# Second MLP matrices: half of the rows by half of the columns of each quarter as seven block products in place of eight

## The chip, the cores and the metric

The kernel runs on one core of a Trainium2 chip. Its time is the device time of one execution in microseconds (us). The engines are TensorE (PE in the profile, with its weight loads PEld beside it), VectorE (DVE), ScalarE (ACT), GpSimd (POOL) and SyncE (SP), which issues the loads. Each works through its own instructions in a fixed order, and waits on the others by semaphores.

## The reference

The reference is a two-layer decoder trunk over 256 tokens of width 2048, in float32: layer 0 has recurrent mixers, layer 1 dilated attention, and each layer ends with an MLP of inner width 8192. The change is in the two MLPs:

```
def squared_relu_mlp(h, w1, w2):
    return jnp.square(jax.nn.relu(h @ w1)) @ w2
...
        h = h + squared_relu_mlp(rms_norm(h, norm_mlp[layer]), mlp_w1[layer], mlp_w2[layer])
```

Here `w1` is 2048 x 8192 and `w2` 8192 x 2048.

## The kernel before

**Precision.** Every large product is made of three passes. A float32 operand is split into `hi`, its rounding to the matmul's type fp32r, and `lo`, the rest, also fp32r; the product is hi x hi + hi x lo + lo x hi. Activations are split by `split_to` (lines 198 to 205), weights by the class `Weights` (85 to 102): ACT casts a half of 1024 columns (line 97) and DVE subtracts it from the raw half (line 98).

**Weight stream.** Weights come in units of 128 x 2048 float32 (1 MB). The list `units` (line 64 on) holds them in the order of use. `unit` (135) hands out the next one and calls `fetch` (104), which issues the load of the unit two further on, on SyncE's queue, and its split. There are three raw tiles (`wraw`, line 46), and five half buffers each for `hi` and `lo` (47, 48). A raw tile is free when its split is done, a half buffer when its last matmul is done.

**The order on the engines.** A scheduler orders every engine's instructions when the program is built: by priority, among those that its own timing says are ready. `stream` moves the loads and splits 150 instructions ahead in priority, `urgent` moves what it encloses 400 ahead (PRIO and URGENT, lines 736 and 737). PE alone keeps the order of the program: `mm` and `turn` (145 to 149) chain every matmul and transpose to the one before.

**The MLP** (`mlp`, line 584) goes by quarters of the inner width, 2048 each. In a quarter, sixteen units of w1 (`project`, 317) give one block of 128 features x 256 tokens each: 16 matmuls of 512 columns and 16 of 256 into one of three PSUM banks "p" (`pmm`, 51). `folded` adds the two halves of the bank, the square of the positive part is taken, and `split_to` writes hi and lo to `bufb[:, m]`. Then come sixteen units of w2, four for each of the four groups n of 512 output columns (`tokens`, 291). There the activations are the stationary operand (128 features x 128 tokens; j is the half of the tokens) and the weights the moving one. A unit has four feature blocks i, two token halves j and three passes: 24 matmuls of 128x512. So a column group takes 96 matmuls into two banks, and a quarter 384. `add_res` (549) then adds each bank, times the token's norm factor, to the residual `xres` on DVE; in the last quarter `Norm.add` takes squares on ACT for the next norm.

**Transposes.** In the last quarter of layer 0, `to_features` (558) appends a job to the list `later`: it transposes the finished 512 columns on PE, four transposes to a bank of the two "pl" banks, which ACT and DVE split with the gain into `bufa`. `flush` (153) runs whatever is in the list, after a unit's matmuls in `tokens` or three quarters through a unit in `project`. With one group finished at a time, eight transposes run at a time.

In layer 1's last quarter the columns are multiplied by the final gain `fing` instead (line 607).

Of the kernel before, what the change touches and what calls it, by code (L numbers as in the profile page):

```python
# [10 lines left out]
F32 = mybir.dt.float32  # L11
F32R = mybir.dt.float32r
# [3 lines left out]
OP = mybir.AluOpType  # L16
# [3 lines left out]
P = 128  # L20
S = 256
D = 2048
KB = D // P
# [17 lines left out]
def trunk_kernel(ctx, tc, x, xtok, cols, tab, masks, pos, fin, w_in, w_gate, w_out, w_qkv, w_o, w1, w2, out):  # L41
    nc = tc.nc
# [33 lines left out]
    for layer in range(2):  # L76
        if layer:
            plan(w_qkv, 48)
            plan(w_o, 16)
        for q in range(4):  # L80
            units.extend((w1, layer * 64 + q * 16 + i) for i in range(16))
            units.extend((w2, layer * 64 + q * 16 + i) for i in range(16))
    at = [0, 0]

    class Weights:
# [18 lines left out]
    def fetch():  # L104
        u = at[0]
        if u >= len(units):
            return
        at[0] += 1
        src, i = units[u]
        with stream():  # L110
            r = wraw.tile([P, 2048], F32, name="raw")
            nc.sync.dma_start(r, src[i])
            made[u] = Weights(r)

    def fetch_first():
        for u in range(4):
# [17 lines left out]

    def unit(src, i):
        u = at[1]
        assert units[u][0] is src and units[u][1] == i, (u, i)
        at[1] += 1
        if u + 2 >= at[0]:
            fetch()  # L140
        return made.pop(u)
# [45 lines left out]

    HA, XA, YA = direct, direct, direct

    def folded(p, name="z", bufs=None):  # L190
        with urgent():
            t = tmp.tile([P, S], F32, name="t1", bufs=2)
            A.copy(t, p[:, S:])  # L193
            z = tmp.tile([P, S], F32, name=name, bufs=bufs)
            V.tensor_tensor(z, p[:, :S], t, OP.add)  # L195
        return z

    def split_to(dst, src, gain=None):
        if gain is None:
            A.copy(dst[:, :S], src)  # L200
            V.tensor_tensor(dst[:, S:], src, dst[:, :S].bitcast(F32), OP.subtract)  # L201
        else:
            A.activation(dst[:, :S], src, AF.Copy, scale=gain)
            V.scalar_tensor_tensor(dst[:, S:], src, gain, dst[:, :S].bitcast(F32),  # L204
                                   op0=OP.mult, op1=OP.subtract)
# [83 lines left out]
            V.scalar_tensor_tensor(r, t, 1.5, r, op0=OP.add, op1=OP.mult)  # L289

    def tokens(src, i0, mov, kgs=(0, 1, 2, 3), by_k=False):
        ps = [pmm.tile([P, 512], F32, name="p") for _ in range(2)]
        for g in kgs:
            w = unit(src, i0 + g)
            order = [(j, i) for i in range(4) for j in range(2)] if by_k else \
                [(j, i) for j in range(2) for i in range(4)]
            for j, i in order:
                k = 4 * g + i
# [239 lines left out]
    for step in ORDER.split():  # L538
# [5 lines left out]
        else:  # L544
            {"x": lru_in, "y": lru_out, "g": lru_gates}[step[0]](i)
    mixers.close()


    def add_res(ps, n, nrm, scale=None):
        at = slice(n * 512, n * 512 + 512)  # L550
        with urgent():
            for j in range(2):
                V.scalar_tensor_tensor(xres[:, j, at], ps[j], 1.0 if scale is None else scale[:, j:j + 1],  # L553
                                       xres[:, j, at], op0=OP.mult, op1=OP.add)
                if nrm:
                    nrm.add(j, n)
# [24 lines left out]
    spot = []  # L581
    spare = cst.tile([P, 1], F32, name="spare")

    def mlp(layer, nrm, nxt, gname):
        r2 = None
        for q in range(4):
            for m in range(16):
                z = folded(project(w1, layer * 64 + q * 16 + m, bufa), "z")
                with urgent():
                    V.scalar_tensor_tensor(z, z, 0.0, z, op0=OP.max, op1=OP.mult)  # L590
                    split_to(bufb[:, m], z)
                if r2 is None:
                    r2 = nrm.inv_mean()
                    if not gname:
                        lut(spare, epsc, AF.Sqrt)
                    spot[:] = [after(V.memset(spare, 0.0), [])]
            for n in range(4):
                ps = tokens(w2, layer * 64 + q * 16 + 4 * n, bufb)
                add_res(ps, n, nxt if q == 3 else None, r2)
                if q == 3:  # L600
                    if gname:
                        to_features(n, gname)
                    else:
                        at = slice(n * 512, n * 512 + 512)
                        with urgent():
                            for j in range(2):
                                V.tensor_tensor(xres[:, j, at], xres[:, j, at], fing[:, at], OP.mult)

    nx1 = Norm()
    mlp(0, nrm, nx1, "nmix1")  # L610


    rot = mixers.enter_context(tc.tile_pool(name="rot", bufs=1))
# [95 lines left out]
    late = ctx.enter_context(tc.tile_pool(name="late", bufs=1))  # L709
    fing = late.tile([P, D], F32, name="fing")  # L710
    nc.sync.dma_start(fing, bass.AP(tensor=fin.tensor, offset=fin.offset, ap=[[0, P], [1, D]]))
    fnorm = Norm()
    mlp(1, nrm, fnorm, None)
    for j in range(2):
# [22 lines left out]
URGENT = 400  # L737
ORDER = "v0 h0 x0 h1 x1 h2 x2 h3 x3 v1 h4 x4 h5 x5 h6 x6 h7 x7 g0 y0 y1 y2 y3 g1 y4 y5 y6 y7"
WARM = 12
NOSYNC = mybir.DependencyInfo(mybir.DependencyClass.NoSync, mybir.DependencyReason.DATA)  # L740


# [23 lines left out]
    return tab, masks  # L766


def _layout(a):
    n = np.asarray  # L770
    blk = lambda w, nb=P: n(w).reshape(w.shape[0] // P, P, w.shape[1] // nb, nb)
# [1 line left out]
    def feat(w):  # L773
        return blk(w).transpose(2, 1, 0, 3).reshape(w.shape[1] // P, P, -1)

    def toks(w):
        b = n(w).reshape(4, 4, P, w.shape[1] // 512, 512)
        return b.transpose(3, 0, 2, 1, 4).reshape(-1, P, 2048)

    colv = lambda v: n(v).reshape(-1, P).T  # L780
# [28 lines left out]
    w2 = np.concatenate([toks(n(w)[q * 2048:q * 2048 + 2048]) for w in a["mlp_w2"] for q in range(4)])  # L809
    tab, masks = _tables()  # L810
    c = np.ascontiguousarray
    return {
# [28 lines left out]
```

## Time and profile before

| what | value |
|---|---|
| median of 3 runs | 2237.01 us (2236.97 to 2237.16) |
| the profiled execution's own time | 2237.57 us |
| its span, first to last instruction | 2235.8 us |
| granted TensorE clock, mean | 0.999 |
| PE busy | 2218.4 us, 99% |
| DVE busy | 1410.6 us, 63% |
| ACT busy | 1074.4 us, 48% |
| loads of raw weights, issue to landing (median) | 4.8 us |
| first MLP, by the windows used below | about 432 to 1142 us |
| second MLP | about 1525 to 2225 us |

A group's row gives the line, the engine, the operation, its output and inputs with shapes, the count, the busy time and the mean length of one, and then the engine's idle time just before such instructions and what ended it. Ends of matmuls are modelled and neighbours overlap, so the distance from one start to the next tells more than the length of one. The chain of waits goes back from the last instruction to what released each step.

### The profile page before, as it was taken

The page shows a single profiled execution, that of the slowest core. Times are in us where ns is not written, and L with a number is a line of the kernel's source. Part 1 is how long each engine was busy: PE and PEld are TensorE (multiplying, and loading weights), DVE is VectorE, ACT ScalarE, POOL GpSimd, SP SyncE. Part 2 cuts the span into 40 slices and gives each one's busy share as a digit, 9 for nine tenths or more (in the row PEclk, how much of TensorE's full clock was granted, in tenths as well). Part 3 has the DMA queues.
Part 4 walks back from the last instruction along what each step waited for, and adds up shares of the span by engine and source line. Part 5 has one row for each costly group of instructions (what it writes and reads, how often), then busy time and mean ns, then how long its engine had stood idle before and what let it go on. Part 6 is the DMA issues. An engine that isn't in the chain of part 4 may idle for free.

```text
span 2235.8 us, 30376 instructions
## 1 busy us (share of the span) xinstructions
PE 2218.4 (99%) x12196; PEld 1935.1 (87%) x12196; DVE 1410.6 (63%) x2220; ACT 1074.4 (48%) x1540; POOL 1.9 (0%) x7
## 2 busy tenths in 40 slices
PE   9999999999999999999999999999999999999998
PEld 8999998888888888888888888888888888888886
DVE  7777886665565565465567878556655645655654
ACT  6444585554444344354554445455434434444543
POOL 0000000000000000000000000000000000000000
PEclk9999999999999999999999999999999999999999
DMA  8444445455555555555554444555555555555553
GB/s 309 151 154 168 152 154 205 172 191 191 200 188 188 190 190 189 199 193 188 188 188 167 172 170 170 191 186 188 189 188 191 191 193 196 189 188 190 190 192 125
DMA packets 58717, 414.51 MB, mean 185 GB/s; under 512 B 6528, under 2 KB 7296, under 8 KB 9168
## 3 DMA queue, kind: packets, MB, share of 16 engines
q1 hardware_dynamic: 58320, 412.20, 51.9%
q8 instruction: 95, 1.56, 0.3%
q0 software_dynamic: 256, 0.38, 0.1%
q14 instruction: 46, 0.38, 0.1%
HBM read 410.70 MB, written 2.10 MB: 185 GB/s over the span
## 4 chain that ended last, share of the span: by engine, by line
PE 98%; ACT 1%; DVE 1%; DMA 0%; issue 0%; SPq 0%; ACTq 0%; DVEq 0%
PE p L146 94%; PE pl L440 1%; PE pl L149 0%; PE pl L665 0%; DMA raw<-in_w_in 0%; PE po L686 0%; PE pd L678 0%; ACT hi L97 0%; DVE bufa L204 0%; ACT L169 0%; DVE lo L98 0%; PE pd L424 0%; PE pl L664 0%; ACT gi L169 0%; PE po L687 0%
## 5 line engine op out<-in xcount | busy, mean ns | idle before, releaser
L98 DVE TENSOR_TENSOR lo<-raw,hi 128x1024 fp32r<-128x1024 f32 (+1 forms) x774 | 932.5, 1220 | 602.7 <-ACT hi L97 435.2
L97 ACT CAST hi<-raw 128x1024 fp32r<-128x1024 f32 (+1 forms) x774 | 811.3, 1049 | 876.7 <-PE p L146 798.7
L146 PE MATMUL p<-bufa,hi 128*128 128x512 f32 (+1 forms) x3840 | 858.2, 357 | 2.4 <-DVE bufa L204 2.4
L146 PE MATMUL p<-hi,bufb 128*128 128x512 f32 x2560 | 792.5, 390 | 0.0
L146 PEld LDWEIGHTS p<-bufa,hi 128*128 128x128 f32 x3840 | 671.9, 189 | 94.8 <-DVE bufa L204 3.5
L146 PEld LDWEIGHTS p<-hi,bufb 128*128 128x128 f32 x2560 | 480.7, 188 | 99.1
L146 PE MATMUL p<-bufa,lo 128*128 128x256 f32 x3200 | 520.0, 284 | 0.0
L146 PE MATMUL p<-lo,bufb 128*128 128x512 f32 x1280 | 498.1, 389 | 0.0
L146 PEld LDWEIGHTS p<-bufa,lo 128*128 128x128 f32 x3200 | 451.9, 191 | 12.3
L146 PEld LDWEIGHTS p<-lo,bufb 128*128 128x128 f32 x1280 | 240.4, 188 | 49.2
L201 DVE TENSOR_TENSOR bufb<-z,bufb 128x256 fp32r<-128x256 f32 x136 | 57.7, 424 | 126.5 <-ACT bufb L200 126.5
L146 PE MATMUL p<-hi,bufa 128*128 128x512 f32 x384 | 122.5, 395 | 0.5 <-ACT hi L97 0.5
L193 ACT COPY t<-p 128x256 f32<-128x256 f32 x128 | 47.6, 372 | 110.0 <-PE p L146 110.0
L146 PEld LDWEIGHTS p<-hi,bufa 128*128 128x128 f32 x384 | 72.2, 188 | 16.1 <-ACT hi L97 1.5
L146 PE MATMUL p<-lo,bufa 128*128 128x512 f32 x192 | 76.4, 398 | 1.6 <-DVE lo L98 1.6
L200 ACT CAST bufb<-z 128x256 fp32r<-128x256 f32 x136 | 54.5, 401 | 17.2 <-DVE z L590 14.4
L553 DVE SCALAR_TENSOR_TENSOR xall<-p,nm,xall 128x512 f32<-128x512 f32 x64 | 47.9, 748 | 19.8 <-PE p L146 19.8
L590 DVE SCALAR_TENSOR_TENSOR z<-z 128x256 f32<-128x256 f32 x128 | 54.5, 426 | 4.4
L195 DVE TENSOR_TENSOR z<-p,t 128x256 f32<-128x256 f32 x128 | 53.5, 418 | 0.0
L258 ACT ACTIVATE z<-xall 128x512 bf16<-128x512 f32 x32 | 20.2, 631 | 53.3 <-DVE xall L553 52.6
L146 PEld LDWEIGHTS p<-lo,bufa 128*128 128x128 f32 x192 | 36.1, 188 | 10.3 <-DVE lo L98 3.6
L440 PE MATMUL pl<-qk 128*128 128x64 f32 x224 | 30.9, 260 | 0.0
(199 smaller groups left out, 730.1 us busy)
## 6 DMA issues: line engine op xcount, KB each, us to landing
raw<-in_w SPq DMA_DIRECT2D x256, 1024.0 KB, 4.8
raw<-in_w_qkv SPq DMA_DIRECT2D x48, 1024.0 KB, 4.8
raw<-in_w_in SPq DMA_DIRECT2D x46, 1024.0 KB, 4.8
raw<-in_w_out SPq DMA_DIRECT2D x16, 1024.0 KB, 4.8
raw<-in_w_o SPq DMA_DIRECT2D x16, 1024.0 KB, 4.8
xall<-in_xtok SPq DMA_DIRECT2D x1, 2048.0 KB, 9.3
raw<-in_w_gate SPq DMA_DIRECT2D x2, 1024.0 KB, 4.8
out<-xall SPq DMA_DIRECT2D x4, 512.0 KB, 3.3
```

Source lines behind the costliest of these rows:

```text
L97: A.copy(h, w)
L98: V.tensor_tensor(l, w, h.bitcast(F32), OP.subtract)
L146: chain[:] = [after(T.matmul(*args, **kw), chain)]
L193: A.copy(t, p[:, S:])
L195: V.tensor_tensor(z, p[:, :S], t, OP.add)
L200: A.copy(dst[:, :S], src)
L201: V.tensor_tensor(dst[:, S:], src, dst[:, :S].bitcast(F32), OP.subtract)
L258: A.activation(q, xres[:, j, n * 512:n * 512 + 512], AF.Square, accum_out=self.ss[:, j, n:n + 1])
L440: T.matmul(pl[:, j], kq[:, js], halves(qp[:, js], c, True), start=True, stop=True)
L553: V.scalar_tensor_tensor(xres[:, j, at], ps[j], 1.0 if scale is None else scale[:, j:j + 1], xres[:, j, at], op0=OP.mult, op1=OP.add)
L590: V.scalar_tensor_tensor(z, z, 0.0, z, op0=OP.max, op1=OP.mult)
```

## The change

In each quarter, the first eight feature blocks (half of the rows of w2) and the first two column groups (half of the columns) are handled together. The activations there are a 2x2 matrix of blocks: two token halves by two sets of four feature blocks, the even ones and the odd ones of the eight (`PAIRED` reorders the rows of w2 accordingly when the inputs are laid out). The weights are a 2x2 matrix as well: two sets of features by two column groups, each block one unit. Their product is made of seven block products of 12 matmuls, by a scheme of Strassen's kind in Winograd's form. The other eight feature blocks of the two groups are multiplied plainly, in four units "n" of 24 matmuls. Groups 2 and 3 stay as they were.

- *Weights.* `plan2` lists eleven operand sets for the pair in the order of `PRODUCTS`; eight load a unit. `combine` makes them. `a` and `t1` are loaded to tiles of their own in the new pool `pair`. DVE then adds in place, in halves of 1024 columns: t1's unit to `a`, then t2's raw unit to `a`, then t2's raw unit to the tile `t1` (t3), then d's raw unit to `a` (t4). Each result is split to hi and lo; `c` is t2's unit split again by itself.
- *Activations.* `sums` makes four sums and differences of each two neighbouring blocks z (DVE, 128x128 each) and splits them into `forms`. The blocks z come from the pool `pair` with three buffers (`zp`).
- *Products.* `products` uses four banks: alpha, delta and gamma of "p", and beta, which is "pd". `after_product` and the ends of the plain units add banks to `xres` by `to_x` on DVE, eight times for the pair where `add_res` made four: beta is added and subtracted in between while its accumulation goes on, and alpha is added to one place after t1 and to another at the end.
- *Transposes.* `to_features` for groups 0 and 1 is called when the pair is complete, so both jobs stand in `later` at the first `flush` of group 2.
- The pool `rot` is opened before the first MLP, since `pair0` comes above it. `T3_DMA` is off.

```diff
@@ the list of units
+    def plan2(i, products):
+        if not products:
+            units.extend((w2, i + u) for u in range(8))
+            return
+        for what, u in PRODUCTS:
+            units.append((w2, None if u is None else i + u, what))
@@ the stream
+    def combine(u, src, i, what):
+        if what in ("a", "t1"):
+            r = held[what] = pair.tile([P, 2048], F32, name=what)
+            nc.sync.dma_start(r, src[i])
+        elif i is not None:
+            r = wraw.tile([P, 2048], F32, name="raw")
+            nc.sync.dma_start(r, src[i])
+            held[what] = r
+        to, add = {"t1": ("a", "t1"), "t2": ("a", "t2"), "t3": ("t1", "t2"), "t4": ("a", "d"),
+                   "a": ("a", None), "c": ("t2", None), "d": ("d", None), "n": ("n", None)}[what]
+        r = held[to]
...
+        for h in range(2):
+            at = slice(h * 1024, h * 1024 + 1024)
+            if add:
+                V.tensor_tensor(r[:, at], r[:, at], held[add][:, at], OP.add)
+            if h == 0:
+                w = made[u] = Weights(r, False)
+            w.split(h * 1024, 1024)
@@ before the MLPs
+    rot = mixers.enter_context(tc.tile_pool(name="rot", bufs=1))
...
+    def sums(k, z1, z2):
+        t = pair.tile([P, 512], F32, name="sums")
+        a11, a21, a12, a22 = z1[:, :P], z1[:, P:], z2[:, :P], z2[:, P:]
+        V.tensor_tensor(t[:, :P], a21, a22, OP.subtract)
+        V.tensor_tensor(t[:, P:2 * P], t[:, :P], a11, OP.subtract)
+        V.tensor_tensor(t[:, 2 * P:3 * P], a11, a21, OP.subtract)
+        V.tensor_tensor(t[:, 3 * P:], a12, t[:, P:2 * P], OP.add)
+        A.copy(forms[:, k, 0], t)
+        V.tensor_tensor(forms[:, k, 1], t, forms[:, k, 0].bitcast(F32), OP.subtract)
+
+    def products(i0, n0, nrm, r2, r2n):
...
+        alpha, delta, gamma = (pmm.tile([P, 512], F32, name="p") for _ in range(3))
+        beta = psc.tile([P, 512], F32, name="po" if n0 else "pd", bufs=1)
...
+        def times(bank, w, get):
+            for i in range(4):
+                h, l = w.part(i * 512, 512)
+                xh, xl = get(i)
+                mm(bank, xh, h, start=not any(b is bank for b in opened), stop=False, skip_group_check=True)
+                opened.append(bank)
+                mm(bank, xh, l, start=False, stop=False, skip_group_check=True)
+                mm(bank, xl, h, start=False, stop=i == 3, skip_group_check=True)
+
+        def to_x(bank, j, n, sign=1, last=False):
+            at = slice(n * 512, n * 512 + 512)
+            with urgent():
+                V.scalar_tensor_tensor(xres[:, j, at], bank, (r2 if sign > 0 else r2n)[:, j:j + 1], xres[:, j, at],
+                                       op0=OP.mult, op1=OP.add)
+                if nrm and last:
+                    nrm.add(j, n)
+
+        after_product = {"a": [(beta, 0, n0, 1)], "t1": [(alpha, 1, n1, 1)], "t2": [(beta, 0, n1, -1)],
+                         "t3": [(beta, 1, n1, -1, True)]}
+        bank = {"a": beta, "t1": alpha, "t2": beta, "c": alpha, "t3": beta, "d": gamma, "t4": beta}
+        for what, u in PRODUCTS:
+            w = unit(w2, None if u is None else i0 + u)
+            if what != "n":
+                times(bank[what], w, side[what])
+                for job in after_product.get(what, ()):
+                    to_x(*job)
+                continue
+            n, g = divmod(u, 4)
+            for j in (1, 0) if n else (0, 1):
+                times({(0, 0): gamma, (0, 1): beta, (1, 0): alpha, (1, 1): delta}[n, j], w,
+                      lambda i, j=j, g=g: plain(j, 4 * g + i))
...
@@ in mlp
-                z = folded(project(w1, layer * 64 + q * 16 + m, bufa), "z")
+                z = folded(project(w1, layer * 64 + q * 16 + m, bufa), "zp", 3, pair)
...
+                if m < 8 and m % 2:
+                    sums(m // 2, zs, z)
+                zs = z
...
             for n in range(4):
-                ps = tokens(w2, layer * 64 + q * 16 + 4 * n, bufb)
-                add_res(ps, n, nxt if q == 3 else None, r2)
+                if n < 2 * PAIRS:
+                    if n % 2 == 0:
+                        products(layer * 64 + q * 16, n, ends, r2, r2n)
+                else:
+                    ps = tokens(w2, layer * 64 + q * 16 + 4 * n, bufb)
+                    add_res(ps, n, ends, r2)
@@ constants
+PAIRS = 1
+T3_DMA = False
+PRODUCTS = (("a", 0), ("t1", 4), ("n", 6), ("t2", 5), ("c", None), ("n", 7), ("t3", None), ("d", 1), ("n", 2),
+            ("t4", None), ("n", 3))
+PAIRED = (0, 2, 4, 6, 1, 3, 5, 7) + tuple(range(8, KB))
```

More of the change, by code (lines that the diff above doesn't have):

```diff
@@ L81, in trunk_kernel @@
             units.extend((w1, layer * 64 + q * 16 + i) for i in range(16))
-            units.extend((w2, layer * 64 + q * 16 + i) for i in range(16))
+            for n in range(0, 4, 2):
+                plan2(layer * 64 + q * 16 + 4 * n, n < 2 * PAIRS)
     at = [0, 0]
@@ L108, in fetch @@
         at[0] += 1
-        src, i = units[u]
+        src, i = units[u][:2]
         with stream():
+            if len(units[u]) > 2:
+                combine(u, src, i, units[u][2])
+                return
             r = wraw.tile([P, 2048], F32, name="raw")
@@ L113, in fetch @@
             made[u] = Weights(r)
+    held = {}
+    def combine(u, src, i, what):
[9 more added lines that the diff above has]
+        r = held[to]
+        if what == "t3" and T3_DMA:
+            nc.gpsimd.dma_start(r, w2[held["c_at"]], accum_op=OP.add)
+            add = None
+        if what == "t2":
+            held["c_at"] = i
+        for h in range(2):
[5 more added lines that the diff above has]
+            w.split(h * 1024, 1024)
     def fetch_first():
@@ L136, in unit @@
         u = at[1]
-        assert units[u][0] is src and units[u][1] == i, (u, i)
+        assert units[u][0] is src and units[u][1] in (None, i), (u, i)
         at[1] += 1
@@ L193, in folded @@
             A.copy(t, p[:, S:])
-            z = tmp.tile([P, S], F32, name=name, bufs=bufs)
+            z = (home or tmp).tile([P, S], F32, name=name, bufs=bufs)
             V.tensor_tensor(z, p[:, :S], t, OP.add)
@@ L291, in tokens @@
     def tokens(src, i0, mov, kgs=(0, 1, 2, 3), by_k=False):
+        ks = PAIRED if src is w2 else range(KB)
         ps = [pmm.tile([P, 512], F32, name="p") for _ in range(2)]
@@ new lines, in products @@
+    def products(i0, n0, nrm, r2, r2n):
+        n1 = n0 + 1
+        i0 += 4 * n0
+        plain = lambda j, k: (bufb[:, k, j * P:j * P + P], bufb[:, k, S + j * P:S + j * P + P])
+        form = lambda f, k: (forms[:, k, 0, f * P:f * P + P], forms[:, k, 1, f * P:f * P + P])
+        side = {"a": lambda i: plain(0, 2 * i), "d": lambda i: plain(0, 2 * i + 1), "t4": lambda i: plain(1, 2 * i + 1),
+                "t1": lambda i: form(0, i), "t2": lambda i: form(1, i), "t3": lambda i: form(2, i),
+                "c": lambda i: form(3, i)}
+        alpha, delta, gamma = (pmm.tile([P, 512], F32, name="p") for _ in range(3))
+        beta = psc.tile([P, 512], F32, name="po" if n0 else "pd", bufs=1)
+        opened = []
+        def times(bank, w, get):
[27 more added lines that the diff above has]
+                      lambda i, j=j, g=g: plain(j, 4 * g + i))
+                if g == 3:
+                    to_x({(0, 0): gamma, (0, 1): beta, (1, 0): alpha, (1, 1): delta}[n, j], j, n + n0, 1, (n, j) != (1, 1))
+            flush()
@@ L591, in mlp @@
                     split_to(bufb[:, m], z)
+                if m < 8 and m % 2:
+                    sums(m // 2, zs, z)
+                zs = z
                 if r2 is None:
                     r2 = nrm.inv_mean()
+                    r2n = tmp.tile([P, 2], F32, name="r2n", bufs=1)
+                    V.tensor_scalar(r2n, r2, -1.0, None, op0=OP.mult)
                     if not gname:
@@ L607, in mlp @@
                                 V.tensor_tensor(xres[:, j, at], xres[:, j, at], fing[:, at], OP.mult)
+    pairs = ExitStack()
+    pair = pairs.enter_context(tc.tile_pool(name="pair0", bufs=1))
+    forms = pair.tile([P, 4, 2, 512], F32R, name="forms")
     nx1 = Norm()
     mlp(0, nrm, nx1, "nmix1")
-    rot = mixers.enter_context(tc.tile_pool(name="rot", bufs=1))
+    pairs.close()
     ppi = rot.tile([32, S], I32, name="ppi")
@@ L711, in trunk_kernel @@
     nc.sync.dma_start(fing, bass.AP(tensor=fin.tensor, offset=fin.offset, ap=[[0, P], [1, D]]))
+    pair = pairs.enter_context(tc.tile_pool(name="pair1", bufs=1))
+    forms = pair.tile([P, 4, 2, 512], F32R, name="forms")
     fnorm = Norm()
     mlp(1, nrm, fnorm, None)
+    pairs.close()
     for j in range(2):
@@ L774, in feat, with toks @@
         return blk(w).transpose(2, 1, 0, 3).reshape(w.shape[1] // P, P, -1)
-    def toks(w):
-        b = n(w).reshape(4, 4, P, w.shape[1] // 512, 512)
+    def toks(w, order=range(KB)):
+        b = n(w).reshape(KB, P, -1)[list(order)].reshape(4, 4, P, w.shape[1] // 512, 512)
         return b.transpose(3, 0, 2, 1, 4).reshape(-1, P, 2048)
@@ L808, in _layout @@
     w1 = np.concatenate([feat(n(w)) for w in a["mlp_w1"]])
-    w2 = np.concatenate([toks(n(w)[q * 2048:q * 2048 + 2048]) for w in a["mlp_w2"] for q in range(4)])
+    w2 = np.concatenate([toks(n(w)[q * 2048:q * 2048 + 2048], PAIRED) for w in a["mlp_w2"] for q in range(4)])
     tab, masks = _tables()
```

5 lines of the change are left out of this document (3 added, 2 removed).

## The prediction

> **What bounds the kernel now.** I read the page's busy times and its chain of waits first, then the busy time by stage in one quarter of the first MLP, then the groups of that stage, then single instructions.
>
> ```profile
> PE 2218.4 (99%) x12196; PEld 1935.1 (87%) x12196; DVE 1410.6 (63%) x2220; ACT 1074.4 (48%) x1540; POOL 1.9 (0%) x7
> PE 98%; ACT 1%; DVE 1%; DMA 0%; issue 0%; SPq 0%; ACTq 0%; DVEq 0%
> ```
>
> TensorE (PE) works nearly all the time and is 98% of the chain that ended last. By stage (window, length, busy PE, PEld, DVE, ACT, POOL, clock, DMA share, GB/s), the first row holds the sixteen units of w1 of a quarter, the second its sixteen units of w2.
>
> ```profile
> 432.00:523.00 91.00, 90.67 (x513) 79.80 (x514) 56.82 (x82) 44.80 (x66) 0.00 (x0) 1.00 0.52 184
> 523.00:610.00 87.00, 87.00 (x393) 72.37 (x392) 44.96 (x41) 34.71 (x34) 0.00 (x0) 1.00 0.54 194
> ```
>
> From the chain in order of time (start, length, what), eight transposes and then 96 matmuls, as many as a column group of w2 has:
>
> ```profile
> 1095.47 0.87 PE pl L149 x8
> 1096.35 21.78 PE p L146 x96
> ```
>
> PE has no idle time in the w2 stage; one matmul of 512 columns takes 21.78 / 96 = 0.2269 us. VectorE (DVE) is busy 45 of 87 us, ScalarE (ACT) 35. What they do there (count, busy us, mean ns, idle before and its releaser):
>
> ```profile
> L98 DVE TENSOR_TENSOR lo<-raw,hi 128x1024 fp32r<-128x1024 f32 x34 | 41.5, 1224 | 42.5 <-ACT hi L97 39.2 <-PE p L146 1.9
> L97 ACT CAST hi<-raw 128x1024 fp32r<-128x1024 f32 x34 | 35.9, 1055 | 53.2 <-PE p L146 51.8 <-DVE z L195 1.5
> L553 DVE SCALAR_TENSOR_TENSOR xall<-p,nm,xall 128x512 f32<-128x512 f32 x8 | 6.0, 748 | 1.6 <-PE p L146 1.6
> ```
>
> ACT waits for PE, and DVE for ACT: the weights are split as far ahead as the five half buffers of each kind allow, two and a half units.
>
> **The matmuls.** The pair of column groups 0 and 1 of a quarter now takes seven products of 12 matmuls and four plain units of 24, 180 in all, where 192 stood. Each of the 12 saved costs 0.2269 us: 2.72 us a quarter, times eight quarters 21.8 us. All of it is on the path, as PE is never idle there. They stay 128x512 on the same kinds of operands, and PE already changes its PSUM bank every 12 matmuls, so I price the rest as before.
>
> [...]
>
> **What VectorE gets in return, in each pair's section.** Two neighbouring operations give the pitch:
>
> ```profile
> 538.82 1.22 DVE L98 TENSOR_TENSOR lo<-raw,hi 128x1024 fp32r<-128x1024 f32 x1 [1.69 <-ACT hi L97]
> 539.96 0.74 DVE L553 SCALAR_TENSOR_TENSOR xall<-p,nm,xall 128x512 f32<-128x512 f32 x1
> 540.62 1.22 DVE L98 TENSOR_TENSOR lo<-raw,hi 128x1024 fp32r<-128x1024 f32 x1
> ```
>
> So 1024 columns occupy DVE 1.14 us and a residual add 0.66. Before, a pair costs 16 splits and 4 residual adds, 20.9 of 43.5 us. After: eleven operand sets, so 22 splits; t1, t2, t3 and t4 each add two halves, 8 adds; eight residual adds for four. No row shows a 128x1024 add with a plain f32 result. At half that width the f32 product with fing (L607) takes 689 ns and the fp32r split (L98) 688, so the type of the result costs nothing; I take 1.14, with the whole duration of 1.22 as the other end. Sum: 30 x 1.14 + 8 x 0.66 = 39.5 us, in a section that PE now crosses in 40.8. This is close (42.0 us at the other end), so I checked it by deadlines.
>
> PE starts the operands at 0 (a), 2.72 (t1), 5.44 (n6), 10.9 (t2), 13.6 (c), 16.3 (n7), 21.8 (t3), 24.5 (d), 27.2 (n2), 32.6 (t4) and 35.4 (n3); second halves are wanted 1.36 later. As now, a, t1 and the first half of n6 can be ready at 0. The first buffer comes free at 1.36. From there DVE must have done, with the residual adds that come due, 1.8 us of work by 6.8 (second half of n6), 5.9 by 10.9 (t2), 11.1 by 16.3 (n7), 16.3 by 21.8 (t3), 22.2 by 27.2 (n2), 29.1 by 35.4 (n3). The least room is 3.6 us, at n6, n7 and n2. Since each half also waits for the half five before it to be used, I followed that too, in the order in which things come due: the tightest is n6's second half, ready at 5.3 and wanted at 6.8. Nothing is late, and at 1.3 us for each split and add nothing is late yet. Cost on the path: zero; if the cover goes, see the rivals. ACT gets 22 casts of 1.06 us, 23 of 40.8.
>
> **The other edits.** The sums of z (four pieces of 128x128, nearest row 291 ns, and a split of 512 columns, 0.69) add 1.9 us of DVE to two w1 units in four of the eight such pairs, where the first stage row leaves 34 of 91 us idle; with ACT's cast of about 0.7 they are hidden. No pass over w1 waits for them: they are first read by t1. Loads stay 8 per pair: a and t1 get buffers of their own, while the raw tile of t2 is kept until t3's add and d's until t4's. The next load in that slot (n2, then two units on) can start only then; behind it stand the later loads on SyncE's queue. A load lands in 4.8 us; t3's adds are done some 7 us before t3 is due, n2 is due 5.4 us after t3: covered by 5 us after splitting. POOL gets nothing. Opening rot earlier and the new pool for z move no work that waits. r2n is one tiny operation per MLP.
>
> **One new wait.** In the last quarter of layer 0, the feature transposes of column groups 0 and 1 now both wait in the list and run together after the first unit of group 2: sixteen, in four lots, on two "pl" banks. Before, eight at a time:
>
> ```profile
> 1095.31 1.03 PE L149 MATMUL pl<-tab__187,xall 128*128 128x128 f32 x8
> ...
> 1096.51 0.83 ACT L203 ACTIVATE bufa<-pl,c__82 128x256 fp32r<-128x256 f32 x2
> ...
> 1097.78 0.87 DVE L204 SCALAR_TENSOR_TENSOR bufa<-pl,c__82,bufa 128x256 fp32r<-128x256 f32 x2
> ...
> 1098.80 0.88 DVE L204 SCALAR_TENSOR_TENSOR bufa<-pl,c__82,bufa 128x256 fp32r<-128x256 f32 x2
> ```
>
> The first bank is free at 1098.65, the second at 1099.68, while PE is through at about 1096.2. So the third lot waits 2.5 us, and the fourth another 0.6 after 0.44 of transposes. PE is held, and the matmuls of group 2 behind it: 3.1 us, once. If DVE takes the bank at once instead of after two splits it is 1.5; behind another two it is 5.4.
>
> **Sum.** The profiled execution took 2237.57 us (span 2235.8), 0.56 above the median of 2237.01. 2237.57 - 21.8 + 3.1 = 2218.9; less 0.56, 2218.3. I say 2218. With the ends of the transposes' wait, and 4 us for small misses, 2214 to 2222.
>
> **Rivals.** *Small holes in every section* (2222 to 2232.5). The t1 product's result is read from alpha and then alpha takes more products; between lie only the 12 matmuls into delta, 2.72 us. One split under way (1.22) and the residual add (0.75) fit. A second operation queued ahead adds 1.14: about 0.5 us late, 4 us over eight sections; two, 13 us. Working value 2218 + 9 = 2227. For: that DVE is 97% occupied. Against: residual adds have the higher priority.
>
> *VectorE becomes the bound* (over 2241.5). Its order is fixed when the program is built, and the trace shows that it keeps it: in the rows above the second split starts when the add is done, though its cast was ready 0.5 us earlier. A split queued behind an add whose operand is late, or an add that stands before a split wanted sooner, uses up the lead. Then each summed weight takes DVE 4 x 1.14 = 4.56 us against 2.72 for its product: 1.84 us late, four times, 7.4 a section, 2.72 saved: 4.6 x 8 = 37 us more, 2255. It decides from 0.68 us of lateness per summed weight. For: 39.5 of 40.8 us. Against: the 3.6 us of room, and no wait of PE for a split in the w2 stage now.
> [...]
>
> *The change gives nothing* (2232.5 to 2241.5), because a matmul costs 7% more in the new order, 0.242 us. No row shows that; PE's bank changes are as frequent now.
>
> **Chances.** Forecast 0.60, small holes 0.14, nothing 0.04, DVE the bound 0.22. About 0.2%, 4.5 us, is what a measurement of this kernel can tell from no change. Faster 0.74, same 0.04, slower 0.22. The predicted time is the likeliest case's, 2218, its own range 2214 to 2222. For 8 in 10 I go from 2214 up through the small holes and the neutral case to 2245, the near end of the DVE case; above lie 0.18, below 0.02.
>
> **What the profile after would show.** 96 fewer matmuls of 512 columns; a pair's section of 40.8 us with PE full and DVE over 90%; a hole of about 3 us ahead of the third lot of transposes near 1084 us. Wrong if PE waits for the splits (L98's successor) or the adds in these sections, or for a residual add ahead of the second plain half of n6.

## The result and the profile after

| | before | after |
|---|---|---|
| median | 2237.07 us (2236.97 to 2237.16) | 2222.99 us (2222.90 to 2223.08) |
| ratio, with its 95% interval | 1 | 0.9937 (0.992 to 0.9954) |
| span of the profiled execution | 2235.8 us | 2221.1 us |
| granted TensorE clock, mean | 0.999 | 0.998 |

The kernel is 14.1 us faster. The forecast was 19, so a quarter of it is missing. The time lies 1.0 us above the forecast's own range (2214 to 2222) and inside the range for 8 in 10 (2214 to 2245).

The page's busy times and its chain of waits, after:

```profile
PE 2201.0 (99%) x12100; PEld 1917.1 (86%) x12100; DVE 1603.2 (72%) x2526; ACT 1142.7 (51%) x1620; POOL 1.9 (0%) x7
PE 97%; ACT 1%; DVE 1%; issue 0%; DMA 0%; SPq 0%; ACTq 0%; DVEq 0%
```

PE runs 96 matmuls fewer (12196 to 12100) and still makes up the chain. DVE's share has gone from 63% to 72%. Next, busy time by stage in the first quarter of the first MLP: the pair's section, then column groups 2 and 3 (window, length, busy PE, PEld, DVE, ACT, POOL, clock, DMA share, GB/s).

```profile
516.20:557.40 41.20, 41.20 (x183) 33.73 (x181) 35.08 (x38) 22.93 (x23) 0.00 (x0) 1.00 0.62 230
557.60:600.70 43.10, 43.10 (x192) 35.67 (x191) 21.96 (x20) 16.77 (x16) 0.00 (x0) 1.00 0.54 195
```

PE is full in the pair's section, and DVE is not: 35.1 of 41.2 us, 85%. But the section takes 41.2 us, not the 40.8 that I forecast. The chain in order of time shows where that is (start, length, what):

```profile
516.38 2.75 PE pd L183 x12
519.13 8.27 PE p L183 x36
527.41 2.80 PE pd L183 x12
530.21 8.24 PE p L183 x36
538.45 2.79 PE pd L183 x12
541.24 5.44 PE p L183 x24
546.68 5.44 PE pd L183 x24
552.12 2.72 PE p L183 x12
```

Read it as lengths divided by counts. The row at 527.41 is the product t2, whose stationary operand is in `forms`: 2.80 / 12 = 0.2333 us for a matmul. The rows from 541.24 on have their stationary operand in `bufb`: 5.44 / 24 = 0.2267, as before the change. The first stretch of 36 is a mixture.

The new wait of the transposes, in the groups of waits of PE and PEld (total, times, longest; in us):

```profile
PE pl L186 <- DVE bufa L241: 3.1, 1, 3.1
PEld p L183 <- DVE xall L657: 1.2, 8, 0.2
```

The first line is 3.1 us, once. The second was not in my sum: the weight load ahead of the second plain product of n6 waits for the residual add that reads `alpha`, in each of the eight sections. The matmuls behind it lose less than these 1.2 us: the stretches at 519.13 and 530.21 above are made up alike (12 matmuls from `forms`, 24 from `bufb`), and the one with the wait takes 8.27 for 8.24. From start to start, the 24 matmuls of n6 lose 0.3 us in all eight sections together. The transposes themselves, in order of time:

```profile
1084.04 1.03 PE L186 MATMUL pl<-tab__187,xall 128*128 128x128 f32 x8
...
1085.23 0.83 ACT L240 ACTIVATE bufa<-pl,c__82 128x256 fp32r<-128x256 f32 x2
...
1086.50 1.89 DVE L241 SCALAR_TENSOR_TENSOR bufa<-pl,c__82,bufa 128x256 fp32r<-128x256 f32 x4
...
1088.15 1.67 PE L186 MATMUL pl<-tab__187,xall 128*128 128x128 f32 x8 [3.08 <-DVE bufa L241]
```

Eight transposes, a hole of 3.08 us, then the other eight. These last take 1.67 us where the first eight took 1.03. The granted clock says why (columns as in the stage rows; the clock is the third number from the end):

```profile
1084.00:1088.00 4.00, 1.07 (x9) 0.79 (x7) 3.72 (x6) 2.65 (x5) 0.00 (x0) 1.00 0.40 115
1088.50:1091.80 3.30, 3.30 (x13) 2.81 (x12) 1.78 (x4) 1.79 (x4) 0.00 (x0) 0.50 0.27 114
1091.90:1096.00 4.10, 4.10 (x20) 3.35 (x19) 0.00 (x0) 0.95 (x1) 0.00 (x0) 1.00 0.00 0
```

For 3.41 us, from 0.3 us after the hole on, PE runs at half its clock, which costs another 1.7 us.

### The profile page after: what moved, and what is told of

Its sections match the earlier page's. It is cut to its first block, busy times and chain, and to the rows that moved or that the text cites. A ratio compares the mean times of both kernels' runs of the same rounds, so it can differ in the third digit from the quotient of the medians.

```text
span 2221.1 us, 30636 instructions
## 1 busy us (share of the span) xinstructions
PE 2201.0 (99%) x12100; PEld 1917.1 (86%) x12100; DVE 1603.2 (72%) x2526; ACT 1142.7 (51%) x1620; POOL 1.9 (0%) x7
## 4 chain that ended last, share of the span: by engine, by line
PE 97%; ACT 1%; DVE 1%; issue 0%; DMA 0%; SPq 0%; ACTq 0%; DVEq 0%
PE p L183 88%; PE pd L183 6%; PE pl L478 1%; PE pl L186 0%; PE pl L774 0%; ACT hi L105 0%; PE po L795 0%; PE pd L787 0%; DMA xall<-in_x 0%; DVE lo L106 0%; DVE bufa L241 0%; ACT L206 0%; ACT bufa L240 0%; PE pd L462 0%; PE pl L773 0%
## 5 line engine op out<-in xcount | busy, mean ns | idle before, releaser
L183 PE MATMUL p<-hi,bufb 128*128 128x512 f32 x1984 | 621.3, 390 | 0.0
L183 PEld LDWEIGHTS p<-hi,bufb 128*128 128x128 f32 x1984 | 373.1, 188 | 78.4 <-DVE xall L657 1.2
L183 PE MATMUL p<-lo,bufb 128*128 128x512 f32 x992 | 386.5, 390 | 0.0
L183 PEld LDWEIGHTS p<-lo,bufb 128*128 128x128 f32 x992 | 186.5, 188 | 38.2
L105 ACT CAST hi<-a 128x1024 fp32r<-128x1024 f32 x64 | 67.3, 1051 | 46.2 <-PE p L183 20.6
L238 DVE TENSOR_TENSOR bufb<-zp,bufb 128x256 fp32r<-128x256 f32 x128 | 54.2, 423 | 47.1 <-ACT bufb L237 41.3
L183 PE MATMUL pd<-hi,bufb 128*128 128x512 f32 x256 | 82.9, 390 | 0.0
L106 DVE TENSOR_TENSOR lo<-a,hi 128x1024 fp32r<-128x1024 f32 x64 | 76.5, 1216 | 0.0
L686 DVE SCALAR_TENSOR_TENSOR zp<-zp 128x256 f32<-128x256 f32 x128 | 54.2, 423 | 3.5
L232 DVE TENSOR_TENSOR zp<-p,t 128x256 f32<-128x256 f32 x128 | 53.3, 416 | 0.0
```

The costliest lines, as they stand in the source:

```text
L105: A.copy(h, w)
L106: V.tensor_tensor(l, w, h.bitcast(F32), OP.subtract)
L183: chain[:] = [after(T.matmul(*args, **kw), chain)]
```

## The experiments

**Theory.** The saving is whole, 21.8 us, and two things take part of it back: the wait of the transposes with its half-clock stretch (4.8 us), and the dearer products from `forms` (384 matmuls by about 6 ns, 2.3 us). DVE takes nothing. `forms` lies 32 bytes off the distance from the weights' buffers that `bufb` has (the addresses in the built programs: `bufb`, `hi` and `lo` all at 320 modulo 512 bytes, `forms` at 288). **Rivals.** The products are dear because of their order and their changes of bank, wherever `forms` lies; or it is DVE that holds the section, and their pitch only shows it.

### Moving `forms` by 32 bytes

```diff
+    pad = pair.tile([P, 8], F32, name="pad")
+    V.memset(pad, 0.0)
     (ahead of forms, for each of the two MLPs)
```

> In the changed kernel the products whose stationary operand comes from forms run at 232 to 233 ns a matmul, those from bufb at 227. In the built program forms starts 32 bytes past a multiple of 64 (byte 182048 of each partition), bufb at a multiple of 64 (69952). Here 32 bytes of padding stand ahead of forms, and nothing else is edited. Theory: the place of the stationary operand sets it. The 384 matmuls from forms fall to 227 ns, and the time falls by 384 x 6.1 ns = 2.3 us, to 2220.7. Rival: they are slow because VectorE and ScalarE are busier in these sections, or because of how the four forms are stored: 233 ns stays, and 2223.0.

Measured: 2219.48 us, ratio 0.9924 (0.9911 to 0.9936). The chain in the pair's section:

```profile
519.07 8.29 PE p L183 x36
527.36 2.72 PE pd L183 x12
530.08 8.16 PE p L183 x36
538.24 2.72 PE pd L183 x12
```

The product t2 at 527.36 now takes 2.72 us, 0.2267 a matmul, and t3 at 538.24 the same. The order of the instructions, the banks and the operands are those of the change, so neither bank nor order made them dear. The time fell by 3.5 us and not by 2.3, because the profiled execution has the 3.1 us hole but no half-clock stretch; of its five times four lie from 2219.40 to 2219.72, and one is 2222.01 (granted clock 0.997, where the four have 0.999). Setting the stretch aside (1.7), the alignment is worth 1.8 us.

The row at 519.07 stays long: 8.29 for 36 matmuls where the next one has 8.16. This is the stretch with the residual add of `alpha` in it, and it explains why 1.8 us came back and not more. The 384 matmuls from `forms` take 87.0 us from start to start here and 89.4 in the change, 2.4 less. But t1 is one of the cheaper products, so n6 wants `alpha` sooner, while DVE's add ends 8.11 us after the section's first matmul in both traces: the 24 matmuls of n6 now lose 0.9 us over the eight sections, where they lost 0.3.

### One job at a time from the list `later`

```diff
-        todo = later[:]
-        later.clear()
+        todo = later[:1]
+        del later[:1]
```

> The changed kernel, but a flush runs one waiting transpose job and not all: the features of column groups 0 and 1 are transposed after two different units, eight at a time as before the change. Theory: the hole of 3.1 us between the second and third lot goes, and with it the one stretch of 3.41 us at half clock that the records show 1.4 us after that hole, worth 1.7 us: 4.8 us less, 2218.2. Rival: the stretch at half clock has another cause and stays: 3.1 us less, 2219.9.

Measured: 2218.29 us, 0.9916 (0.9902 to 0.993), 4.7 us under the change. The chain around the place:

```profile
1078.85 5.44 PE p L183 x24
1084.29 0.87 PE pl L186 x8
1085.16 5.46 PE p L183 x24
1090.62 0.87 PE pl L186 x8
```

Eight transposes, a unit's matmuls, the other eight: no hole, full clock. The wait and its stretch are worth 3.08 + 1.71 = 4.8 us, and 4.7 came back, so the stretch goes with the hole. It begins 0.3 us after the hole's end, not 1.4 as the expectation has it.

### Both together

> The changed kernel with both edits at once: the 32 bytes of padding ahead of forms, and one transpose job a flush. If the two losses are separate they add up: 2223.0 - 4.7 (as the second run gave) - 2.3 = 2216.0. The whole gain of the saved matmuls over the kernel before, 21.8 us of 2237.0, would be 2215.2; what is then still missing, under 1 us, is not in the matmuls' rate or the transposes.

Measured: 2216.21 us (2216.11 to 2216.50), 0.9908 (0.9891 to 0.9924). The two losses add. What is left to the full saving (2237.0 - 21.8 = 2215.2) is 1.0 us, 0.13 in each section. That is the difference between the rows 8.29 and 8.16 above, which stand in this run's chain too: the wait for `alpha`'s residual add, which takes 0.9 us from the matmuls of n6 in this trace.

### The kernel before, with `bufb` moved

```diff
+    pad0 = act.tile([P, 8], F32, name="pad0")
     bufb = act.tile([P, KB, 2 * S], F32R, name="bufb")
+    pad1 = act.tile([P, 8], F32, name="pad1")
     (both set to zero on DVE)
```

> The kernel before the change, with 32 bytes of padding ahead of bufb and 32 behind it, so that bufb alone starts 32 bytes past a multiple of 64 and all else keeps its place to a multiple of 64. Theory of the place: the 3840 matmuls of 128x512 with a stationary block of bufb go from 226.8 to about 233 ns: 3840 x 6.1 ns = 23 us more, 2260. Rival (business of the engines, or the form of the buffer): no change, 2237.0.

Measured: 2256.06 us, 1.0084 (1.0069 to 1.01): 19.0 us slower from two pads of 32 bytes, with no other instruction changed than the two that set them to zero, which are new. From start to start, a w2 matmul went from 0.2267 to 0.2333 us, as those from `forms` in the change. For the 8 x 384 of them that makes 20.3 us; w1's stage gave back 0.28 in each of the eight quarters (below), so 18.1 are accounted for. The expectation of 2260 counted all 3840 matmuls with a stationary block of `bufb`; they did take 25.3 us more in the trace, but the matmuls with `bufa` streaming took 7.2 less, which it had not foreseen. The second pad moves everything behind `bufb` by 64 bytes, the weights' buffers too; so `bufb` lies 32 bytes off them, and `bufa` 64.

That second part tells something I hadn't asked. In w1's stage `bufa` streams and the weights are stationary. Before:

```profile
461.44 3.82 PE L146 MATMUL p<-bufa,hi 128*128 128x512 f32 x16
465.10 2.08 PE L146 MATMUL p<-bufa,lo 128*128 128x256 f32 x16
467.01 3.82 PE L146 MATMUL p<-bufa,hi 128*128 128x512 f32 x16
```

and with the pads:

```profile
464.57 3.89 PE L150 MATMUL p<-bufa,hi 128*128 128x512 f32 x16
468.29 1.98 PE L150 MATMUL p<-bufa,lo 128*128 128x256 f32 x16
470.11 3.89 PE L150 MATMUL p<-bufa,hi 128*128 128x512 f32 x16
```

From start to start, the matmuls of 512 columns went from 3.66 / 16 = 0.2288 to 0.2325 us, but those of 256 columns from 1.91 / 16 = 0.1194 to 0.1138. The stage as a whole, from a quarter's first w1 matmul to its first w2 matmul, was no slower (89.04 before, 88.76 after). So at 64 bytes the wide matmuls were dearer, and the narrow ones cheaper.

### Everything moved, and other distances

The kernel before with a pad of 32 bytes behind the constants, so that all later tiles move alike:

```diff
+    pad = cst.tile([P, 8], F32, name="pad")
+    V.memset(pad, 0.0)
```

> The kernel before the change with 32 bytes of padding at the end of the pool of constants, so that every later tile (bufa, bufb, hi, lo, raw) starts 32 bytes past a multiple of 64, and their distances are as they were. If only the address of the stationary operand matters, the 128x512 matmuls from bufb go to 233 ns as in the run with bufb alone shifted, and the time is at least 2256. If the place of the stationary operand relative to the moving one matters, nothing changes: 2237.

Measured: 2237.08 us, 1.0001 (0.9991 to 1.001). Moved by 32 bytes together, the tiles cost nothing, where `bufb` put 32 bytes off the weights' buffers cost 19.0 us; in these runs it is the distance from the stationary operand to the other buffers that counted. Which other one is in part an inference: in the run with `bufb` moved, all buffers behind it moved alike. But its w2 matmuls in the first MLP took 0.2332 to 0.2335 us on average, whether DVE or ACT worked beside them or not, so I take it to be the moving operand. Which distances are dear was asked of the change, with pads of 96 and of 160 bytes ahead of `forms` in place of 32; these leave it 64 and 128 bytes off.

> The changed kernel with 96 bytes of padding ahead of forms: it then starts at a multiple of 128 (byte 182144), while the moving weights start 64 past a multiple of 128, and bufb as well. If a multiple of 64 is what the stationary operand needs, forms runs at 227 ns as with 32 bytes, 2220.0 (2219.5 without the stretch at half clock, 2222 with it). If it must share the moving operand's place within 128 bytes or more, forms stays at about 233 ns and the time at 2223.0 (2220.5 without that stretch).

> The changed kernel with 160 bytes of padding ahead of forms. Its distance to the buffers of hi is then 128 more than a multiple of 256 and of 512, where 32 bytes of padding gave a multiple of 512 (226.7 ns), 96 bytes 64 past a multiple of 128 (233.3), and none 96 past (232.9). If the two operands must agree within 128 bytes, forms runs at 227 ns here; if within 256 or more, at 233.

Measured: 2222.66 us (2221.91 to 2223.42), 0.9936, and 2224.67 us (2223.21 to 2225.07), 0.9943. The products t2 and t3 with 96 bytes:

```profile
527.44 2.80 PE pd L183 x12
530.24 8.27 PE p L183 x36
538.51 2.80 PE pd L183 x12
```

That is 0.2333 us again, and 0.2325 to 0.2333 with 160 bytes. So 32, 64 and 128 bytes off are all dear, and among the distances tried only the multiple of 512 was cheap; 256 was not tried. Why is not shown. The times of the two kernels differ mainly by the half-clock stretch: the profiled execution with 96 bytes (2221.96) has none, the one with 160 (2224.57) has one of 6.83 us.

### Adds made twice: how much room has DVE?

The change, where each add of weights is first made into a scratch tile that nobody reads:

```diff
             if add:
+                V.tensor_tensor(scr, r[:, at], held[add][:, at], OP.add)
                 V.tensor_tensor(r[:, at], r[:, at], held[add][:, at], OP.add)
```

> The changed kernel, with each of the eight adds of 128x1024 in a section made twice, the first time into a scratch tile that nobody reads. VectorE then has 39.5 + 8 x 1.14 = 48.6 us of work in a section of 41.2. Theory (the change is near the point at which VectorE becomes the bound; the least lead of a split in the trace is 1.3 us): the leads are used up and PE waits. About 6 us of the 9.1 can't be had from the lead, so roughly 5 us a section, 40 us in all: 2263. Rival (VectorE has room, as its busy share of 72% over the span would suggest): within 5 us of 2223.

Measured: 2261.51 us (2259.97 to 2265.15), 1.0111 (1.0098 to 1.0125). The time is as expected, the place is not. The waits of PE:

```profile
PE p L184 <- DVE xall L658: 25.1, 8, 3.1
...
PE p L184 <- DVE lo L106: 2.9, 6, 0.8
```

PE hardly waits for splits; it waits for one residual add, eight times 3.1 us. DVE's order in the first section shows it:

```profile
524.36 1.21 DVE L148 TENSOR_TENSOR t<-t,raw 128x1024 f32<-128x1024 f32 x1
525.50 1.22 DVE L147 TENSOR_TENSOR scr<-t,raw 128x1024 f32<-128x1024 f32 x1
526.63 0.41 DVE L687 SCALAR_TENSOR_TENSOR zp<-zp 128x256 f32<-128x256 f32 x1
526.97 0.74 DVE L658 SCALAR_TENSOR_TENSOR xall<-p,nm,xall 128x512 f32<-128x512 f32 x1
```

`alpha`'s product t1 is over at 521.7, but its add to the residual starts at 526.97, behind the adds for t3, which no one needs for more than 10 us. In the change itself the same add is the tightest point: in the fifth section it begins at 1785.67 and ends at 1786.41, and the weight load that waits for it is 0.15 us late.

```profile
1784.20 1.21 DVE L106 TENSOR_TENSOR lo<-a,hi 128x1024 fp32r<-128x1024 f32 x1
1785.33 0.41 DVE L686 SCALAR_TENSOR_TENSOR zp<-zp 128x256 f32<-128x256 f32 x1
1785.67 0.74 DVE L657 SCALAR_TENSOR_TENSOR xall<-p,nm,xall 128x512 f32<-128x512 f32 x1
```

The sum of this kernel: 25.1 us of holes (28.5 by the weight loads), and in the profiled execution seven half-clock lengths of 3.41 us, in which PE stood idle for 1.55 us anyway, so 11.2 lost: 36.3 to 39.7, where that execution (2260.66) lies 39.5 above the change without its stretch (2222.90 - 1.71). That the expectation's 2263 came so near is luck: it had the waits at the splits, and no half clock.

### The scheme for both pairs of column groups

Both mends, and the seven products for groups 2 and 3 as well, whose section then follows the first pair's at once and can prepare nothing during w1:

```diff
-PAIRS = 1
+PAIRS = 2
```

> As the run before it in this list, with PAIRS = 2: column groups 2 and 3 go through products too, so another 96 matmuls are saved and VectorE has 79 us of work in a w2 stage of 82. Theory (VectorE is then the bound there, because no plain group is left in which it catches up): part of the second 21.8 us is lost in waits of PE for residual adds and splits at the head of the second section, about 1 us a quarter and a stretch at half clock where a hole is long: 2216 - 21.8 + 8 to 20 = 2202 to 2214. Rival (the lead still suffices): 2194. Rival (VectorE's waits eat more than the second pair saves): over 2216.

Measured: 2219.03 us (2217.44 to 2219.15), 0.9918 (0.9904 to 0.9933): 2.8 us more than with one pair, where the matmuls alone would give 2194.4. The theory's 2202 to 2214 is missed; the rival over 2216 came true. The stage of a quarter, and the waits of PE:

```profile
516.00:601.20 85.20, 82.63 (x364) 67.31 (x363) 74.71 (x75) 45.73 (x46) 0.00 (x0) 1.00 0.58 210
```

```profile
PE p L183 <- DVE lo L106: 9.7, 17, 1.3
PE p L183 <- DVE xall L657: 7.5, 8, 1.0
```

DVE is busy 74.7 of 85.2 us, and PE now has idle time, for splits and for residual adds, at the head of the second section. So the rival "VectorE becomes the bound" is true of the second pair; the first escapes it because part of its DVE work is done during w1 (below). Up to 1.6 us of the time are the clock's: near the end of the profiled execution two holes of 1.28 and 0.98 us, 1.4 us apart, are followed by 3.41 us at half clock.

To take load from DVE, the add for t3 can be made by the load itself, an adding DMA on POOL's queue, which loads t2's unit a second time:

```diff
-T3_DMA = False
+T3_DMA = True
```

> Both pairs by products, as in the run that gave 2219.0, but t3's sum is made by a load that adds into the tile t1 (GpSimd's queue) and not by VectorE: 2.28 us a section less for VectorE, 74.4 us in a w2 stage of 81.6. In the trace of that run PE's waits lie at t1 and n6 of the second section alone (least lead of a split 0.05 us there, 3.2 us at t3). Theory (what counts is the lead at the head of a section, which the five half buffers bound, and not VectorE's total): t3 was not short of time, so little changes, 2215 to 2219. Rival (VectorE's total work sets it): the 24.6 us lost against 2194.4 shrink by most of 16 x 2.28 = 36 us: 2194 to 2203.

Measured: 2213.40 us (2213.33 to 2214.17), 0.9895 (0.9879 to 0.9912), below the theory's range and far from the rival's. Two adds fewer per section give back 5.6 us, of which up to 1.6 are the stretch at half clock, which this profiled execution does not have. What remains is mostly `xall`, grown from 7.5 to 11.1 while the splits fell from 9.7 to 3.5:

```profile
PE p L183 <- DVE xall L657: 11.1, 15, 1.0
PE p L183 <- DVE lo L106: 3.5, 5, 1.3
```

The next step puts another product between t1 and n6, so that `alpha`'s residual add has 5.4 us and not 2.7:

```diff
-PRODUCTS = (("a", 0), ("t1", 4), ("n", 6), ... ("t3", None), ("d", 1), ("n", 2),
+PRODUCTS = (("a", 0), ("t1", 4), ("d", 1), ("n", 6), ... ("t3", None), ("n", 2),
```

> The run before (both pairs by products, t3 by an adding load, 2213.4), with the product d moved from behind t3 to behind t1. Then 24 matmuls lie between t1's product and the next matmul into alpha, and not 12; beta's room after t3 falls to 12, at a place where the splits have 3 us of lead. In the run before PE waited for the residual add of alpha in 15 of 16 sections, with its weight loads held 17.8 us in total, and 7.5 us for splits. Theory (the short room for alpha's residual add is the main wait): most of its share goes, 10 to 14 us: 2199 to 2204. Rival (VectorE is simply full at the head of a section, and the wait moves to a split): 2210 to 2214.

Measured: 2206.56 us (2204.72 to 2206.84), 0.9861 (0.9845 to 0.9878), the fastest kernel of this case. PE's longest waits:

```profile
PE p L183 <- DVE lo L106: 7.9, 14, 1.2
```

The wait for `xall` is gone; that for splits has grown from 3.5 to 7.9. So 6.8 us came back and not the 9 to 14 that the theory said, nor the rival's 3 or less: the gain lies between. The same order with the add for t3 back on DVE:

> The same order of products, with t3's sum by VectorE again, to be read against the run that gave 2219.0 (both pairs, d behind t3). There PE's weight loads were held 12.9 us by residual adds of alpha and 18.9 us by splits. Theory: the first share goes, 8 to 12 us: 2207 to 2211. Rival: the splits' waits take its place: 2217 to 2219.

Measured: 2224.36 us (2223.57 to 2224.57), 0.9943 (0.9928 to 0.9957), 5.3 us worse than the old order under the same load (2219.03), against both expectations.

```profile
PE p L183 <- DVE lo L106: 20.7, 27, 1.3
```

The order alone doesn't help. Of PE's waits in this run 16.3 us lie within t1's product of the second sections, where the old order lost 3.4. DVE there has one of the adds for t3, which nobody needs yet, ahead of each half of t1's split, in both orders; in the first quarter t1's own adds begin 1.5 us later in the new one (at 556.05, after 554.52). With the adds for t3 gone from DVE the same order is a gain. Why the builder puts t1's adds later is not shown.

## Why the prediction was right or wrong

**The matmuls: right in their number, mis-sized in their price.** 96 went, and PE is still the chain. The step "they stay 128x512 on the same kinds of operands ... so I price the rest as before" failed: the 384 matmuls with `forms` as the stationary operand took 0.2325 to 0.2333 us, not 0.2269. Undoing that took 2.4 us from these matmuls, and 1.8 from the kernel. I had looked at kinds of operands and banks, not at addresses, and the trace of before, with one distance throughout the w2 stage, could not show that they matter.

**The wait of the transposes: right in its cause and size, 3.08 us where I had 3.1.** Its two steps were not as I had them. The first bank was free at 1087.37, but the third lot started only at 1088.15, 0.15 us after the first half of the second bank was done, and the fourth lot then had no wait of its own. That the totals agree so closely is luck. What I left out is what came after this hole: half clock for 3.41 us, 1.7 more. No stage row of before that I read had a clock below 1.00.

**DVE: its load was overstated, its tightest place was mis-named, and "Cost on the path: zero" was off by 0.3 us here, and by 1.0 with `forms` mended.** I counted all eight adds within the section. In the first quarter's trace five of them start before it, during the last two w1 units: both of t1, one of t2, both of t3. An add needs its loads and, in `a`, the split of the sum before; it needs no half buffer. That leaves 35.1 us where I had 39.5, and 85% where I had over 90%. The tightest split had 1.3 us to spare (c's), near my 1.5 (for n6's second half). But the tightest operation of all was `alpha`'s residual add, the one on which I built the rival of small holes. The weight load behind it is 0.15 us late in each section, 1.2 us together, and the matmuls lose 0.3 of that: under a tenth of the 4 us at which that rival began. It is the sign of being wrong that I had named, a residual add ahead of the second plain half of n6, at a small price. "Against: residual adds have the higher priority" did not protect it: two operations stood ahead of it in DVE's fixed order (rows at 1784.20 and 1785.33).

**The rest of the sum.** Forecast 2218.3; plus 2.4 for `forms`, 1.7 for the clock, 0.3 for `alpha`: 2222.7, measured 2223.0. For the last 0.3 us I have no cause. The sums of z and the loads cost nothing that can be seen.

**The rivals.** Small holes: the mechanism exists, at 0.04 us a section (0.13 with `forms` mended). That the result (2223.0) falls into its numbers is chance: 4.1 of the 4.7 us between forecast and result have other causes. VectorE as the bound: not with one pair; with two pairs it takes back more than the second pair saves. Its price was mis-summed: 37 us more than the kernel before is 2274 us, and 2255 counts the saving twice. A matmul dearer in the new order: half right. It is dearer by 2.5 to 3% (0.2325 to 0.2333 after 0.2267), in 384 matmuls, and not because of the order, as the same order with 32 bytes more shows.

## What to carry to other kernels

When a change gives a matmul a new operand buffer, compare its distance in bytes from the other operand with that of a buffer that is known to be fast, and time 12 matmuls of each in the chain: a pad of 32 bytes was worth 1.8 us here, and two of them cost 19 us in the kernel before. Price a hole of PE not by its length alone: look at the granted clock behind it (one of 3.08 us cost 4.8 here), and add up holes that lie close together (two of 1.28 and 0.98 us, 1.4 us apart, were followed by 3.41 us at half clock in one execution). And when an engine's order is fixed, look for the small operation queued behind large ones that nobody needs yet: here it held the path, and doubling the large ones measured its room (25.1 us of waits in eight sections).

## What the runs showed of the hardware

**Distance of the operands.** A 128x512 fp32r matmul with a new stationary block each time took 0.2267 us when the stationary operand lay a multiple of 512 bytes from the moving one, and 0.2325 to 0.2333 when it lay 32, 64 or 128 bytes off it (256 was not tried; that the moving operand is the one that counts is in part an inference). Moving both alike by 32 bytes changed nothing (2237.08 after 2236.94 us). With the operands' roles exchanged and 64 bytes between, the 512-column ones were dearer (0.2325 after 0.2288), and the 256-column ones cheaper (0.1138 after 0.1194).

**Half clock after a hole.** In the change's trace the granted clock falls at 1088.45 us, rises at 1091.87 and falls for good at 2214.85: 1.0 and 329.0 steps of 3.413 us from one to the next. In five profiled executions (the change, the pads of 32, 96 and 160 bytes, the doubled adds) I laid a grid of this step, counted back from the last fall of each, over the 13 holes of PE of 3.08 and 3.14 us. Where 1.99 us of the hole or more fell into one step of the grid, the next step ran at half clock (8 of 13); where no step had more than 1.93, the clock stayed (5 of 13). The ends of matmuls are modelled, so the two figures are not sharp. In two of the eight the step after ran at half clock too; in these 0.97 and 1.09 us of the hole lay in the first half-clock step itself, in the others 0.46 at most. In one execution two holes did it together: with both pairs by products and t3 on DVE, in the old order, they put 1.26 and 0.73 us into one step, and the next ran at half clock. So the same hole cost 3.1 us (pad of 32 bytes), 4.8 (the change) or more (160 bytes, two steps at half clock) by its phase, and the kernel with the pad of 32 bytes, whose profiled execution had the hole astride two steps, took 2219.4 to 2219.7 us four times and 2222.0 once.

**An adding load.** The 1 MB load that adds to its tile, on POOL's queue, landed in 8.1 us (median), where plain 1 MB loads of weights on SyncE's queue took 4.8 to 5.3 in the same execution (both pairs by products, t3's sum by the load).
